# The first weight tile and x block loaded by halves from two queues, one token square on VectorE, and the up weights of two pairs kept and loaded ahead of four stores

## The chip, the core and the metric

The kernel runs on one core of a Trainium2 chip. The core has TensorE (PE in the profile; its weight loads are PEld), VectorE (DVE), ScalarE (ACT), GpSimd (POOL) and SyncE (SP), which run their own instruction streams and wait for each other by semaphores. 16 DMA engines move data for the core; SyncE and ScalarE hand them transfers through hardware queues, GpSimd through a software queue, which here carries all accumulating transfers. The metric is the device time in microseconds; lower is better. Times are medians of several runs; the profile is of one execution.

## The reference, cut to what matters

One layer of a decoder trunk over 1024 tokens of 1024 channels, in float32:

```python
h = rms_norm(x, g_mix)
z = h @ w_in + b_in                        # 1024 x 7168
va, ga, xb, gb, sa, sb = split(z)
u = silu(layer_norm(causal_conv31(va * sigmoid(ga))))
y_a = u @ w_a_out
v = rg_lru(causal_conv4(xb))
y_b = (v * gelu(gb)) @ w_b_out
x = x + (sigmoid(sa) * y_a + sigmoid(sb) * y_b) @ w_o
h = rms_norm(x, g_mlp)
f = square(relu(h @ w_1))                  # w_1: 1024 x 4096
x = x + f @ w_2
out = rms_norm(x, g_final)
```

The change touches two places: the first matmuls of `h @ w_in` with the norm ahead of them, and the passage from `@ w_o` to `h @ w_1`.

## The kernel before

**Split products.** A float32 operand is split in a high part h (rounded to the fast matmul type by a copy on ScalarE) and a low part l (the rest, by a subtraction on VectorE or by an accumulating transfer from GpSimd). A product takes three matmuls: hh, lh and hl. `split_dma` (L63) makes the low part with ScalarE (L65), an accumulating DMA on GpSimd's queue (L66) and a second ScalarE copy (L67).

**The start (L115 to L405).** Tokens come in two halves of 512 (hf 0 and 1), channels in eight blocks of 128 (c or k from 0 to 7). `xc` holds x transposed: one tile per half and pair of blocks, 512 KB each, so that `xc[0]` has the blocks 0 and 1 of the first half. `xt` holds x by tokens, eight tiles of 128 tokens, numbered t = 0 to 7; the tiles 4 to 7 (the second half) are loaded and squared first. `raw0` are the first three weight tiles (column blocks 16, 0 and 8 of w_in), 512 KB each. SyncE issues, in order: gmix (the norm's gains, 4 KB), `raw0[0]`, four tiles of xc, two more weight tiles, four of xt, four of xc, four of xt (L130 to L172). A DMA takes one of eight semaphore lanes, and the ninth waits until the first has landed.

The order on ScalarE, VectorE and TensorE is written out by hand inside `manual_schedule` (L336 to L403). TensorE runs spare passes (`idle_mm`), then for the first token half, block by block, the three products of weight tile 0. ScalarE makes the high part of each block with gmix as scale (`x_plain`, L227), VectorE the low part (`x_plain_low`, L231). Then TensorE runs weight tiles 1 and 2 on the same half. Meanwhile the tokens of the second half are squared and summed (`x_square`, L195), from which `x_root` (L202 to L210) makes 1/rms and writes it on diagonals `rd`, and four matmuls spread it over the partitions (`x_spread`, L217). That spread stands in TensorE's order behind the fifth block of weight tile 2. `x_scaled` (L221, L222) then scales the second half by it. In between VectorE works off a chain of small steps on 12 columns, the decay rates of the recurrence (`decay`, a generator; `decay_on(n)` runs n steps of it). The first half is multiplied unscaled and gets its 1/rms afterwards.

**From w_o to w_1 (GX and useq, L1773 to L1860).** Matmuls there follow Strassen-like seven-product schemes over four pairs of column blocks. `gseq` lists the steps (weight, pair i, product p): 28 for `w_a_out`, 28 for `w_o`, and, with weight "u", the products 1 and 2 of the up projection for the pairs 0 to 3 (`AHEAD` = 4); `u0` = 56 is the place of the first of those. `GX` says what else is issued at each step. After this loop `useq` runs the other up products (L1709). The weights of pair i are two raw tiles of 512 KB, `raws[i, 0]` and `raws[i, 1]`, loaded by `up_load` on SyncE (L1664). Products 1 and 2 need only `raws[i, 0]`; `g_lhs` reads it and, behind product 2, deletes the entry for the pairs 2 and 3. The loop over `useq` loads what isn't there when a pair's product 6 comes near.

In that passage GpSimd's queue carries the low parts `gu` of the up products 1 and 2 and then `o` of the others; SyncE's queue carries `x1d` (the residual, stored by rows, L1585), then the stores `fd<-f` of product 2's results (L1486), which wait for ScalarE, and the up loads.

Of the kernel before, what the change touches and what calls it, by code (L numbers as in the profile page):

```python
# [30 lines left out]
def trunk_kernel(ctx: ExitStack, tc: tile.TileContext, x, xt_in, xt_eo, vecs, w_in, w_a_out, w_b_pl, w_b_sq,  # L31
                 w_rg, w_o, w_1, w_2, g_final, out):

    nc = tc.nc
# [19 lines left out]
    HALVES = (slice(0, HS), slice(HS, S))  # L54


    def load_w(w, name):

        raw = wp.tile(list(w.shape), F32, tag="raw", name=name + "_raw")
        nc.sync.dma_start(raw, w)  # L60
        return raw
# [56 lines left out]
    wp = stage.enter_context(tc.tile_pool(name="weights", bufs=2))  # L118
# [8 lines left out]
    vec = cp.tile([P, 448], F32, name="vec")  # L127

    gmix = cp.tile([P, 16], F32, name="gmix")
    nc.sync.dma_start(gmix[:, 0:8], vecs[:, 0:8])  # L130
    nc.gpsimd.dma_start(vec, vecs)
    gmix_c = gmix[:, 0:8]
    bin_c = vec[:, 8:64]
# [11 lines left out]
    xt, xc, raw0 = [], [], []  # L145
# [6 lines left out]
    def load_xc(hf, c2):  # L152
        a = T(f"xc{hf}{c2}")
        nc.sync.dma_start(a, xt_in[hf, c2])
        xc.append(a)

    def load_w0(i):
        if i < 2:
            raw0.append(load_w(w_in[(16, 0, 8)[i]], f"w{i}"))
        else:  # L160
            raw0.append(T(f"w{i}_raw").rearrange("p (k c) -> p k c", c=P))
            nc.sync.dma_start(raw0[i], w_in[(16, 0, 8)[i]])

    load_w0(0)
    for c2 in range(4):
        load_xc(0, c2)
    load_w0(1)
    load_w0(2)
# [12 lines left out]
    def xpart(a, hf, c):  # L181
        return a[hf][c // 2][:, HALVES[c % 2]]

    rs_x = {}

    def x_square(t, eng):

        hf, i = divmod(t, 4)
        if hf not in rs_x:
            rs_x[hf] = cp.tile([P, 5, 4], F32, tag="st4", name=f"stx{hf}", bufs=2)  # L190
        a, ss = xt[(t + 4) % 8], rs_x[hf][:, 0, i:i + 1]
        if eng is nc.vector:
            nc.vector.scalar_tensor_tensor(a, a, 1.0, a, ALU.mult, ALU.mult, accum_out=ss)
        else:
            nc.scalar.activation(a, a, AF.Square, accum_out=ss)  # L195
# [16 lines left out]
    def x_spread(hf):  # L212

        rb[hf] = rb["tile"][:, HALVES[hf]]
        for i in range(4):
            d = slice(i * P, (i + 1) * P)
            nc.tensor.matmul(rb[hf][:, d], ones, rb["d"][:, d], start=True, stop=True)  # L217
# [6 lines left out]
    def x_plain(c):  # L224

        u = xc[c // 2][:, HALVES[c % 2]]
        nc.scalar.activation(xpart(xh, 0, c), u, AF.Copy, scale=gmix_c[:, c:c + 1])  # L227

    def x_plain_low(c):
        u, h = xc[c // 2][:, HALVES[c % 2]], xpart(xh, 0, c)  # L230
        nc.vector.scalar_tensor_tensor(xpart(xl, 0, c), u, gmix_c[:, c:c + 1], h.bitcast(F32),  # L231
                                       ALU.mult, ALU.subtract)
# [8 lines left out]
    w0 = []  # L241

    def first_w(i, part):
        if part == "h":
            if i < 2:
                wh = wp.tile([P, 8, P], F32R, tag="wh", name=f"w{i}_h")
                wl = wp.tile([P, 8, P], F32R, tag="wl", name=f"w{i}_l")
            else:
                wh, wl = (T(f"w{i}_{n}", F32R).rearrange("p (k c) -> p k c", c=P) for n in "hl")
            w0.append((wh, wl))  # L250
            z0.append(PS(f"z{16 + i}"))
            nc.scalar.activation(wh, raw0[i], AF.Copy)
        else:
            nc.vector.tensor_tensor(w0[i][1], raw0[i], w0[i][0].bitcast(F32), ALU.subtract)

    def first_z(i, hf, k, which):
        w, a = {"hh": (0, xh), "lh": (1, xh), "hl": (0, xl)}[which]
        nc.tensor.matmul(z0[i][:, HALVES[hf]], w0[i][w][:, k, :], xpart(a, hf, k),  # L258
                         start=k == 0 and which == "hh",
                         stop=k == 7 and which == ("hl" if i == 0 else "lh"))  # L260
# [69 lines left out]
    def decay_on(n=99):  # L330

        for _ in range(n):
            next(decaying, None)

    with tc.manual_schedule(engines={mybir.EngineType.Activation, mybir.EngineType.DVE,
                                     mybir.EngineType.PE}):  # L336
        warm = cp.tile([P, 10], F32, name="warm")
        nc.vector.memset(warm[:, 0:2], 1.0)
        nc.scalar.activation(warm[:, 0:1], warm[:, 1:2], AF.Sqrt)

        spare = PS("spare", "ps2")

        def idle_mm(n):
            for _ in range(n):
                nc.tensor.matmul(spare[:, 0:P], ones, ones, start=True, stop=True)

        idle_mm(13)
        rb["tile"] = PS("rb", "ps2")
        first_w(0, "h")
        first_w(0, "l")  # L350
        for c in range(8):
            x_plain(c)
            x_plain_low(c)
            if c == 7:
                first_w(1, "h")
                first_w(1, "l")
            for which in ("hh", "lh", "hl"):
                first_z(0, 0, c, which)
        for k in range(8):
            first_z(1, 0, k, "hh")  # L360
            first_z(1, 0, k, "hl")
        decay_on(6)
        first_w(2, "h")
        first_w(2, "l")
        decay_on(14)
        for t in range(4, 8):
            x_square(t, nc.scalar)
        for k in range(8):
            first_z(1, 0, k, "lh")
        x_root(1)  # L370
        decay_on(5)
        for k in range(8):
            first_z(2, 0, k, "hh")
            first_z(2, 0, k, "hl")
            if k == 4:
                x_spread(1)
        for k in range(8):
            first_z(2, 0, k, "lh")

        for c in range(9):  # L380
            if c < 8:
                x_scaled(1, c)
            else:
                x_root(0)
                x_spread(0)
            if 3 <= c < 7:
                x_square(c - 3, nc.scalar)
            if c:
                for which in ("hh", "lh"):
                    first_z(0, 1, c - 1, which)  # L390
                x_low(1, c - 1)
                first_z(0, 1, c - 1, "hl")
                for i in range(1, N0):
                    first_z(i, 1, c - 1, "hh")
                    first_z(i, 1, c - 1, "hl")
        for i in range(1, N0):
            for k in range(8):
                first_z(i, 1, k, "lh")
        decay()
# [295 lines left out]
    def later(ready, cost, f, *a):  # L695

        todo.append((ready, len(todo), cost, f, a))
# [89 lines left out]
    for i in range(2, NZ):  # L787
        n = zseq.index((i, 1))
# [20 lines left out]
    with tc.manual_schedule(engines=ENGINES):  # L809
        for s in range(3, NC1):  # L810
# [30 lines left out]
            c = CH[s - 1]  # L841
# [27 lines left out]
            for d in range(5):  # L869
                if s - d in EXP:  # L870
# [6 lines left out]
                    t = 3 * g + d - (2 if g < 3 else 1)  # L877
# [21 lines left out]
    wp = stage.enter_context(tc.tile_pool(name="weights2", bufs=3, reuse_waits="tile"))  # L899
# [123 lines left out]
    with tc.manual_schedule(engines=ENGINES):  # L1023
# [159 lines left out]
        for n in range(len(zseq) + 2):  # L1183
# [9 lines left out]
            if n + 3 < len(zseq):  # L1193
                i, p = zseq[n + 3]
# [15 lines left out]
    wp = early.enter_context(tc.tile_pool(name="weights3", bufs=7, reuse_waits="tile"))  # L1210
# [191 lines left out]
    def g_lhs(w, i, p):  # L1402
        if w == "u":
            src = raws[i, 0][:, 4 * (p - 1):4 * p, :]
            if p == 2 and i > 1:
                del raws[i, 0]
        elif p in (5, 6):
            src = gs[w, i][p - 5 and 1]
        else:
            src = graw[w, i, {1: 0, 2: 1, 3: 1, 7: 0, 4: 1}[p]][:, int(p == 4)]  # L1410
        go[w, i, p] = o = T(f"g{w}{i}_{p}", F32R).rearrange("p (x k c) -> p x k c", x=2, c=P)
        if w == "a" and p in (1, 2, 7):
            nc.scalar.activation(o[:, 0], src, AF.Copy)
# [242 lines left out]
    raws = {}  # L1656
# [113 lines left out]
    def g_get(n, f):  # L1770
# [32 lines left out]
        0: ((up_lhs, 0, 6), (x1_rows, 4, 5, 6, 7)),  # L1803
        1: ((x1_diag, 1),), 2: ((x1_spread, 1), (up_lhs, 1, 6)),
        3: ((x1_normed, 0, 1), (x1_normed, 1, 1), (g_t, "u", 0, 1), (g_t, "u", 1, 1)),
        4: ((g_t, "u", 0, 2), (g_t, "u", 1, 2)), 5: ((g_parts, "u", 6, 0),),
        6: ((g_parts, "u", 6, 1), (g_parts, "u", 5, 0), (up_lhs, 0, 5)),
        7: ((g_parts, "u", 5, 1), (up_lhs, 1, 5), (g_t, "u", 0, 3), (g_t, "u", 1, 3))}.items()})
    BX = {}
# [147 lines left out]
    with tc.manual_schedule(engines={mybir.EngineType.Activation, mybir.EngineType.DVE,  # L1957
                                     mybir.EngineType.PE}):
        for n in range(len(useq)):
# [4 lines left out]
            while ready < min(len(useq), n + look + 1):  # L1964
                i, p = useq[ready]
# [167 lines left out]
    with tc.manual_schedule(engines={mybir.EngineType.Activation, mybir.EngineType.DVE,  # L2133
                                     mybir.EngineType.PE}):
        for n, (g, p, kk) in enumerate(dseq[:-2]):
# [41 lines left out]
            if (g, m - 4) in XADD:  # L2177
                k = XADD[g, m - 4]
# [103 lines left out]
```

## Time and profile before

| | |
|---|---|
| median of 3 runs | 1531.3 us (1531.1 to 1531.85) |
| profiled execution, its own time | 1531.15 us |
| profiled execution, its span | 1529.4 us |
| TensorE busy, share of the span | 1519.5 us, 99% |
| granted TensorE clock, mean | 0.999 |
| DMA share of the 16 engines, 0 to 22 us | 0.92 |

The span runs from the first to the last instruction of the profiled execution; its own time has what lies around it too. A timeline row gives start and duration in us, the engine, the line, the operation, the tile written and the tiles read; in brackets stands how long the engine had been idle and what ended that. "SPq" is SyncE issuing a transfer, not the transfer. A row with x4 merges four instructions that follow each other, with the time from the first's start to the last's end. A wait for several semaphores is put down to the last.

### The profile page before, as it was taken

Reading aid. Unit: us, or ns where it says so; the run is one execution under the profiler, and the core shown is the slowest. Engines: PE = TensorE matmul, PEld = TensorE weight load, DVE = VectorE, ACT = ScalarE, POOL = GpSimd, SP = SyncE. Lnnn points to the kernel's source line nnn. Section 1 sums busy time; section 2 is a strip of 40 time slices with the busy share of each in tenths; the row PEclk is TensorE's granted clock in tenths of the full one; section 3 lists DMA queues with packets and bytes.
Section 4 is the critical chain, followed back from the end, with each engine's and each line's share of the span. In section 5 each row is a group of like instructions: output and inputs, shape, how many; then the busy total and the mean of one; then the engine's idle time right before and its main releaser. Section 6 shows DMA issues by size and latency. Waiting matters only on the chain.

```text
span 1529.4 us, 18963 instructions
## 1 busy us (share of the span) xinstructions
PE 1519.5 (99%) x6722; PEld 1251.2 (82%) x6722; DVE 1200.0 (78%) x1636; ACT 928.3 (61%) x1299; POOL 192.3 (13%) x228
## 2 busy tenths in 40 slices
PE   9999999999999999999999999999999999999998
PEld 7878887888888888888888887888888888888886
DVE  6899996998999997788869879755555387777777
ACT  6748688576566667645575777554444455545475
POOL 0111011022222222000022332000000000101010
PEclk9999999999999999999999999999999999999999
DMA  9766779797997889964879897333333974776465
GB/s 352 188 146 154 184 159 204 196 258 209 265 261 173 186 207 271 297 226 119 269 201 302 188 205 195 138 122 111 111 111 111 302 265 131 177 211 169 107 123 153
DMA packets 130799, 296.53 MB, mean 194 GB/s; under 512 B 12896, under 2 KB 34912, under 8 KB 130704
## 3 DMA queue, kind: packets, MB, share of 16 engines
q1 hardware_dynamic: 98960, 215.92, 42.0%
q0 software_dynamic: 31600, 79.15, 28.1%
q8 instruction: 52, 0.85, 0.2%
q14 instruction: 43, 0.35, 0.1%
q10 hardware_dynamic: 144, 0.26, 0.0%
HBM read 149.79 MB, written 60.82 MB: 138 GB/s over the span
## 4 chain that ended last, share of the span: by engine, by line
PE 96%; issue 2%; DVE 1%; POOL 1%; DMA 0%; ACT 0%; POOLq 0%; ACTq 0%
PE z L725 16%; PE z L258 2%; PE d1b L2002 2%; PE d2b L2002 2%; PE d0b L2002 2%; PE d3b L2002 2%; PE d0e L2002 1%; PE d3e L2002 1%; PE d3a L2002 1%; PE d2e L2002 1%; PE d2a L2002 1%; PE d1e L2002 1%; PE d1a L2002 1%; PE d0a L2002 1%; PE rg L532 1%
## 5 line engine op out<-in xcount | busy, mean ns | idle before, releaser
L725 PE MATMUL z<-xh,win_h 128*128 128x512 f32 x368 | 115.4, 391 | 0.0
L725 PE MATMUL z<-xl,win_h 128*128 128x512 f32 x368 | 114.9, 390 | 0.0
L637 DVE SCALAR_TENSOR_TENSOR y<-u,vec,y 128x511 f32<-128x511 f32 (+14 forms) x120 | 88.2, 735 | 0.0
L725 PE MATMUL z<-xh,win_l 128*128 128x512 f32 x368 | 87.4, 389 | 0.0
L637 DVE SCALAR_TENSOR_TENSOR yt<-u,vec,yt 128x511 f32<-128x511 f32 (+6 forms) x112 | 82.5, 736 | 0.0
L637 DVE SCALAR_TENSOR_TENSOR y<-yt,csum,y 128x511 f32<-128x511 f32 (+6 forms) x112 | 82.4, 736 | 0.0
L725 PEld LDWEIGHTS z<-xh,win_h 128*128 128x128 f32 x368 | 69.1, 188 | 16.0 <-ACT win_h L67 0.5
L725 PEld LDWEIGHTS z<-xl,win_h 128*128 128x128 f32 x368 | 69.1, 188 | 14.9
L725 PEld LDWEIGHTS z<-xh,win_l 128*128 128x128 f32 x368 | 69.1, 188 | 14.6
L542 ACT ACTIVATE g<-rg,vec 96x1024 f32<-96x1024 f32 x32 | 35.5, 1110 | 72.9 <-PE rg L534 72.8
L1697 ACT ACTIVATE o<-s 128x512 fp32r<-128x512 f32 x56 | 33.7, 623 | 45.7 <-DVE s L1681 26.4
L66 POOL DMA_DIRECT2D zo<-zw x45 | 39.2, 871 | 133.8 <-ACT zo L65 110.4
L483 DVE SCALAR_TENSOR_TENSOR v<-xb,vec,v 128x1023 f32<-128x1023 f32 (+2 forms) x36 | 46.2, 1282 | 6.3 <-ACT v L474 5.3
L66 POOL DMA_DIRECT2D db_10l<-br x4 | 3.5, 877 | 339.6 <-DMA br<-in_w_dram 254.4
L66 POOL DMA_DIRECT2D win_l<-win_raw x23 | 20.0, 868 | 194.0 <-ACT win_l L65 155.9
L65 ACT ACTIVATE zo<-zw 128x512 fp32r<-128x512 f32 x45 | 28.2, 626 | 24.3 <-PE z10f L929 2.1
L1219 DVE TENSOR_TENSOR o<-s,o 128x512 fp32r<-128x512 f32 x56 | 37.2, 683 | 1.3 <-ACT o L1697 1.3
L66 POOL DMA_DIRECT2D zo<-zs x30 | 26.4, 879 | 75.9 <-ACT zo L65 63.8
L67 ACT ACTIVATE zo<-zw 128x512 fp32r<-128x512 f32 x45 | 27.9, 621 | 0.0
L578 DVE TENSOR_TENSOR_SCAN g<-a,g 128x1024 f32<-128x1024 f32 x12 | 27.5, 2291 | 0.4
L66 POOL DMA_DIRECT2D ga<-gsa x8 | 7.0, 874 | 161.0 <-DMA m<-mbd 150.8
L1219 DVE TENSOR_TENSOR o<-w_raw,o 128x512 fp32r<-128x512 f32 x38 | 25.9, 683 | 0.0
(3182 smaller groups left out, 4912.0 us busy)
## 6 DMA issues: line engine op xcount, KB each, us to landing
w_raw<-in_w_dram SPq DMA_DIRECT2D x34, 512.0 KB, 5.7
br<-in_w_dram SPq DMA_DIRECT2D x32, 512.0 KB, 6.1
ar<-fd SPq DMA_DIRECT2D x32, 512.0 KB, 7.0
zw<-in_w_in_dram SPq DMA_DIRECT2D x28, 512.0 KB, 6.9
win_raw<-in_w_in_dram SPq DMA_DIRECT2D x23, 512.0 KB, 5.0
win_l<-win_raw POOLq DMA_DIRECT2D x23, 512.0 KB, 5.2
zo<-zw POOLq DMA_DIRECT2D x45, 256.0 KB, 5.7
gates<-zg SPq DMA_DIRECT2D x32, 256.0 KB, 4.1
```

The lines of the kernel that those rows point to most:

```text
L65: nc.scalar.activation(l, src, AF.Copy, scale=-1.0)
L66: nc.gpsimd.dma_start(l, src, accum_op=ALU.add)
L67: nc.scalar.activation(h, src, AF.Copy)
L258: nc.tensor.matmul(z0[i][:, HALVES[hf]], w0[i][w][:, k, :], xpart(a, hf, k), start=k == 0 and which == "hh", stop=k == 7 and which == ("hl ...
L483: nc.vector.scalar_tensor_tensor(v[:, d:S], a[:, 0:S - d], cbw_c[:, w * 12 + t:w * 12 + t + 1], v[:, d:S], ALU.mult, ALU.add)
L542: nc.scalar.activation(a, gps.pop((n, gi))[:HD, :], AF.Sigmoid, bias=(ba_c, bx_c)[gi][:, n:n + 1])
L578: nc.vector.tensor_tensor_scan(i, a, i, 0.0, ALU.mult, ALU.add)
L637: nc.vector.scalar_tensor_tensor(o[:, k:], a[:, 0:HS - k], c, o[:, k:], ALU.mult, add)
L725: nc.tensor.matmul(zps[s][:, HALVES[hf]], w[:, k, :], xw[k][part][hf], start=n == 0, stop=n == 23)
L1219: tt(l, src, h.bitcast(F32), ALU.subtract)
L1697: nc.scalar.activation(o[:, 0], src, AF.Copy)
L2002: nc.tensor.matmul(o, a, b, start=start and n == 0, stop=stop and n == len(todo) - 1, skip_group_check=not start or not stop)
```

## The change

Five edits, in the diff below:

1. gmix is no longer SyncE's first transfer. `raw0[0]` and `xc[0]` are loaded in halves (256 KB each): SyncE issues the first half of the weight tile, gmix, and the second half of the x block; ScalarE's queue the first half of the x block and the second half of the weight tile.
2. The high and low parts of weight tile 0 are made by halves (`first_half`): the first before the blocks, the second behind the high and low part of block 2.
3. 9 calls of spare matmuls in place of 13 (each is two passes in the profile).
4. Of the four token squares ahead of `x_root(1)`, t = 6 runs on VectorE; all four stand ahead of 14 steps of the decay chain, not behind them.
5. `raws[2, 0]` and `raws[3, 0]` are kept, and `raws[2, 1]` and `raws[3, 1]` are loaded at step u0 + 4, so that the loop over `useq` loads neither pair.

```diff
@@ consts, first loads
-    nc.sync.dma_start(gmix[:, 0:8], vecs[:, 0:8])
     nc.gpsimd.dma_start(vec, vecs)
...
-    load_w0(0)
-    for c2 in range(4):
+    raw0.append(wp.tile([P, 8, P], F32, tag="raw", name="w0_raw"))
+    xc.append(T("xc00"))
+    nc.sync.dma_start(raw0[0][:, 0:4], w_in[16, :, 0:4])
+    nc.scalar.dma_start(xc[0][:, HALVES[0]], xt_in[0, 0, :, HALVES[0]])
+    nc.sync.dma_start(gmix[:, 0:8], vecs[:, 0:8])
+    nc.scalar.dma_start(raw0[0][:, 4:8], w_in[16, :, 4:8])
+    nc.sync.dma_start(xc[0][:, HALVES[1]], xt_in[0, 0, :, HALVES[1]])
+    for c2 in range(1, 4):
         load_xc(0, c2)
@@ first_w, first_half
-            nc.scalar.activation(wh, raw0[i], AF.Copy)
+            if i:
+                nc.scalar.activation(wh, raw0[i], AF.Copy)
...
+    def first_half(n):
+        k = slice(4 * n, 4 * n + 4)
+        h, l = (a[:, k] for a in w0[0])
+        nc.scalar.activation(h, raw0[0][:, k], AF.Copy)
+        nc.vector.tensor_tensor(l, raw0[0][:, k], h.bitcast(F32), ALU.subtract)
@@ the written order
-        idle_mm(13)
+        idle_mm(9)
         rb["tile"] = PS("rb", "ps2")
         first_w(0, "h")
-        first_w(0, "l")
+        first_half(0)
         for c in range(8):
             x_plain(c)
             x_plain_low(c)
+            if c == 2:
+                first_half(1)
...
         first_w(2, "l")
+        for t in range(4, 8):
+            x_square(t, t == 6)
         decay_on(14)
-        for t in range(4, 8):
-            x_square(t, nc.scalar)
@@ g_lhs
             src = raws[i, 0][:, 4 * (p - 1):4 * p, :]
-            if p == 2 and i > 1:
-                del raws[i, 0]
@@ GX, step u0 + 4
-        4: ((g_t, "u", 0, 2), (g_t, "u", 1, 2)), 5: ((g_parts, "u", 6, 0),),
+        4: ((up_load, 2, (1,)), (up_load, 3, (1,)), (g_t, "u", 0, 2), (g_t, "u", 1, 2)), 5: ((g_parts, "u", 6, 0),),
```

How the instructions stand, at three places. First ScalarE at the start: `w_raw` is the raw weight tile, `w_h` its high part, `xc` the x block and `xh` its high part. Before:

```order
L339 ACT_TABLE_LOAD
L339 ACTIVATE warm<-warm 128x1
L252 ACTIVATE w_h<-w_raw 128x1024
L227 ACTIVATE xh_129<-xc_93,gmix 128x512 x2
L227 ACTIVATE xh_130<-xc_95,gmix 128x512 x2
L227 ACTIVATE xh_131<-xc_97,gmix 128x512 x2
L227 ACTIVATE xh_132<-xc_99,gmix 128x512 x2
L252 ACTIVATE w_h<-w_raw 128x1024 x2
```

And now:

```order
L166 DMA xc_91<-in_xt_dram 128x512
L168 DMA w_raw<-in_w_in_dram 128x512
L351 ACT_TABLE_LOAD
L351 ACTIVATE warm<-warm 128x1
L265 ACTIVATE w_h<-w_raw 128x512
L232 ACTIVATE xh_131<-xc_91,gmix 128x512 x2
L232 ACTIVATE xh_132<-xc_97,gmix 128x512
L265 ACTIVATE w_h<-w_raw 128x512
L232 ACTIVATE xh_132<-xc_97,gmix 128x512
L232 ACTIVATE xh_133<-xc_99,gmix 128x512 x2
L232 ACTIVATE xh_134<-xc_101,gmix 128x512 x2
L258 ACTIVATE w_h<-w_raw 128x1024 x2
```

Two DMA issues stand ahead of the table load, and half of the weight copy has moved behind the first high part of the second x tile.

Second VectorE where the token square comes in: `sm` is the decay chain, `w_l` the low part of weight tile 2, `x` a token tile and `stx` its sum of squares. Before:

```order
L284 TENSOR_SCALAR sm<-sm 128x12
L254 TENSOR_TENSOR w_l<-w_raw,w_h 128x1024
L286 SCALAR_TENSOR_TENSOR sm<-sm 128x12
L288 SCALAR_TENSOR_TENSOR sm<-sm 128x12
L290 MEMSET sm 128x12
```

And now:

```order
L296 TENSOR_SCALAR sm<-sm 128x12
L260 TENSOR_TENSOR w_l<-w_raw,w_h 128x1024
L198 SCALAR_TENSOR_TENSOR x_111,stx_247<-x_111 128x1024
L298 SCALAR_TENSOR_TENSOR sm<-sm 128x12
L300 SCALAR_TENSOR_TENSOR sm<-sm 128x12
L302 MEMSET sm 128x12
```

The square stands ahead of fourteen `sm` steps, and behind those, in both, the first step of the root (L202, now L207). On ScalarE one of four squares is gone.

Third SyncE's queue at the passage to the MLP: `x1d` is the residual by rows, `fd` the up projection's results, `w_4_raw` and `w_5_raw` the raw tiles of pair 2, `w_6_raw` and `w_7_raw` those of pair 3. Before:

```order
L1585 DMA x1d<-x1r_7845 128x1024
L1585 DMA x1d<-x1r_7863 128x1024
L1486 DMA fd<-f_0_7992 128x512
L1486 DMA fd<-f_1_8012 128x512
L1486 DMA fd<-f_2_8040 128x512
L1486 DMA fd<-f_3_8066 128x512
L1664 DMA w_4_raw<-in_w_dram 128x1024
L1664 DMA w_5_raw<-in_w_dram 128x1024
L1664 DMA w_6_raw<-in_w_dram 128x1024
L1766 DMA fd<-fa_8152 128x512
L1664 DMA w_7_raw<-in_w_dram 128x1024
L1664 DMA w_8_raw<-in_w_dram 128x1024
```

And now:

```order
L1597 DMA x1d<-x1r_7845 128x1024
L1597 DMA x1d<-x1r_7863 128x1024
L1676 DMA w_5_raw<-in_w_dram 128x1024
L1676 DMA w_7_raw<-in_w_dram 128x1024
L1498 DMA fd<-f_0_7996 128x512
L1498 DMA fd<-f_1_8016 128x512
L1498 DMA fd<-f_2_8044 128x512
L1498 DMA fd<-f_3_8070 128x512
L1676 DMA w_8_raw<-in_w_dram 128x1024
L1778 DMA fd<-fa_8156 128x512
```

Two loads stand ahead of the stores in place of four behind them; the second loads of `w_4_raw` and `w_6_raw` are gone. On TensorE and GpSimd nothing has moved but the spare matmuls that were dropped.

More of the change, by code (lines that the diff above doesn't have):

```diff
@@ L184, in trunk_kernel, with x_square @@
     rs_x = {}
-    def x_square(t, eng):
+    def x_square(t, dve=False):
         hf, i = divmod(t, 4)
@@ L191, in x_square @@
         a, ss = xt[(t + 4) % 8], rs_x[hf][:, 0, i:i + 1]
-        if eng is nc.vector:
+        if dve:
             nc.vector.scalar_tensor_tensor(a, a, 1.0, a, ALU.mult, ALU.mult, accum_out=ss)
@@ L386, in trunk_kernel @@
             if 3 <= c < 7:
-                x_square(c - 3, nc.scalar)
+                x_square(c - 3)
             if c:
```

## The prediction

> **What bounds the kernel now.** I read the page first, then the waits of TensorE's weight loads, then the timeline of the two stretches that the change touches.
>
> ```profile
> span 1529.4 us, 18963 instructions
> PE 1519.5 (99%) x6722; PEld 1251.2 (82%) x6722; DVE 1200.0 (78%) x1636; ACT 928.3 (61%) x1299; POOL 192.3 (13%) x228
> ...
> PE 96%; issue 2%; DVE 1%; POOL 1%; DMA 0%; ACT 0%; POOLq 0%; ACTq 0%
> ```
>
> TensorE is busy for 1519.5 of 1529.4 us and makes up 96% of the chain that ended last. A microsecond counts where TensorE waits, or where the change makes it wait, and almost nowhere else. These are its waits in the two places (line, what ended the wait, us in total, times, longest):
>
> ```profile
> PEld f0d L1709 <- DMA o<-s: 1.2, 1, 1.2
> PEld z L258 <- DVE xl L231: 0.8, 2, 0.5
> PEld rb L217 <- PE z L258: 0.5, 1, 0.5
> ...
> PEld gu1a L1427 <- DMA gu<-w_raw: 0.3, 1, 0.3
> ```
>
> Three are in the first 23 us, two in the step from the output projection to the MLP's up projection (near 925 and 945 us). Besides them only the wait for the first real matmul, filled with spare passes, can be won. This is the start, as the timeline has it (start, us, engine, line; in brackets the idle time before and what ended it):
>
> ```profile
> 0.74 0.39 SPq L130 DMA_DIRECT2D gmix<-in_vecs_dram  x1
> 1.18 0.42 SPq L60 DMA_DIRECT2D w_raw<-in_w_in_dram  x1
> 1.60 5.92 PE L345 MATMUL spare<-ones 128*128 128x128 f32 x26 [1.60 <-POOL ones L113]
> 4.95 1.06 ACT L252 ACTIVATE w_h<-w_raw 128x1024 fp32r<-128x1024 f32 x1 [2.72 <-DMA w_raw<-in_w_in_dram]
> 6.34 1.33 ACT L227 ACTIVATE xh<-xc,gmix 128x512 fp32r<-128x512 f32 x2 [0.34 <-DMA xc<-in_xt_dram]
> 7.17 0.70 PE L258 MATMUL z<-xh,w_h 128*128 128x512 f32 x1
> 8.12 3.88 ACT L227 ACTIVATE xh<-xc,gmix 128x512 fp32r<-128x512 f32 x6 [0.44 <-DMA xc<-in_xt_dram]
> 8.88 4.07 DVE L231 SCALAR_TENSOR_TENSOR xl<-xc,gmix,xh 128x512 fp32r<-128x512 f32 x6 [0.29 <-ACT xh L227]
> ...
> 15.17 1.22 DVE L254 TENSOR_TENSOR w_l<-w_raw,w_h 128x1024 fp32r<-128x1024 f32 x1
> 16.31 0.17 DVE L286 SCALAR_TENSOR_TENSOR sm<-sm 128x12 f32<-128x12 f32 x1
> 17.09 1.06 ACT L195 ACTIVATE x<-x 128x1024 f32<-128x1024 f32 x1 [0.15 <-DMA x<-in_x_dram]
> 18.36 1.06 ACT L195 ACTIVATE x<-x 128x1024 f32<-128x1024 f32 x1
> 18.80 0.17 DVE L293 TENSOR_TENSOR sm<-sm 128x12 f32<-128x12 f32 x1
> 19.33 0.18 ACT L195 ACTIVATION_READ_ACCUMULATOR x<-x 128x1 f32 x1
> 19.54 0.17 DVE L202 TENSOR_SCALAR stx<-stx 128x4 f32<-128x4 f32 x1 [0.58 <-ACT x L195]
> 20.98 0.39 PE L258 MATMUL z<-xl,w_h 128*128 128x512 f32 x1
> 21.47 0.97 PEld L217 LDWEIGHTS rb<-rd,ones 128*128 128x128 f32 x8 [0.52 <-PE z L258]
> ```
>
> Two things are to be seen. Transfers pace the start: ScalarE waits for x blocks at 6.34 and 8.12 and for a token square at 17.09. And at 21.47 TensorE, done with its matmuls, waits for the root of the token squares (L202 to L210), whose spread (L217) stands in its order. So what counts in the first 23 us is when that root starts, 19.54 now; 21.47 − 19.54 = 1.93 us later the spread runs. Matmuls that start earlier only wait longer there.
>
> **The start, part by part.** Gone are 0.44 us (1.18 − 0.74) in which SyncE issued the small gmix ahead of the first big transfer, and eight of the 26 spare passes (5.92/26 = 0.23 us each; 18 end near 5.7). ScalarE's queue issues two halves before its table load, where it has nothing else to do. I shift all later landings by 0.44: bytes and order stay the same. The first real matmul then comes near 5.7, not 7.17. It does not last: the second x block lands at 8.12 − 0.44 = 7.68. There the second half of the weight copy stands behind the third high part on ScalarE, and its low part on VectorE.
>
> ```profile
> L65 ACT ACTIVATE zo<-zw 128x512 fp32r<-128x512 f32 x45 | 28.2, 626 | 24.3 <-PE z10f L929 2.1
> L1219 DVE TENSOR_TENSOR o<-s,o 128x512 fp32r<-128x512 f32 x56 | 37.2, 683 | 1.3 <-ACT o L1697 1.3
> L483 DVE SCALAR_TENSOR_TENSOR v<-xb,vec,v 128x1023 f32<-128x1023 f32 (+2 forms) x36 | 46.2, 1282 | 6.3 <-ACT v L474 5.3
> ```
>
> ScalarE: 7.68 + 3.88 (six high parts) + 0.63 (the half copy, first row) = 12.2, before 8.12 + 3.88 = 12.0. VectorE ends its six low parts 0.95 behind ScalarE now (8.88 + 4.07 = 12.95), so near 13.1. The copy that was hidden in the wait for the x block is no longer hidden, and eats what the earlier transfers gave.
>
> Now the token square. VectorE goes from its last low part (12.95) to the end of w_l at 15.17 + 1.22 = 16.39 in 3.44 us; from 13.1 that is 16.6. The third token tile landed just before 17.09, with the shift 16.63. The square on VectorE costs about 1.28 (third row, the same operation on 1023 columns): 17.9. Then come the fourteen small steps of the decay chain, 18.80 + 0.17 − 16.31 = 2.66 us, which in the old order ran while ScalarE squared: 20.6. ScalarE has its three squares by 18.36 − 0.44 + 1.06 + 0.18 = 19.2, 0.3 earlier than now (19.33 + 0.18), and waits. The root starts at 20.6 instead of 19.54: **+1.1 us**. Bounds: without any shift of the transfers 21.0 (+1.5); with a shift of 0.9, since two queues may fill the engines sooner, the sum on VectorE gives about 20.1 (+0.6).
>
> Behind the spread nothing gives it back:
>
> ```profile
> 23.45 1.29 ACT L222 ACTIVATE xh<-xc 128x512 fp32r<-128x512 f32 x2 [1.70 <-DVE xc L221]
> 25.66 0.39 PE L258 MATMUL z<-xh,w_h 128*128 128x512 f32 x1
> ```
>
> TensorE needs this first high part (ready near 24.1) at 25.66, and both start from the spread; they move together.
>
> **The step to the MLP.** Two loads (the second halves of pairs 2 and 3) are issued before the four stores of fd, two reloads are dropped, and three loads leave the stretch behind 938.
>
> ```profile
> 915.02 2.29 SPq L1585 DMA_DIRECT2D x1d<-x1r  x2
> 917.24 0.95 POOL L66 DMA_DIRECT2D gu<-w_raw  x1 [5.90 <-ACT gu L65]
> ...
> q1 hardware_dynamic: 428, 1.57, 100.3%
> ...
> q0 software_dynamic: 6, 0.01, 0.9%
> ...
> 937.92 7.48 DMA o<-s
> ...
> 938.81 6.63 SPq L1664 DMA_DIRECT2D w_raw<-in_w_dram  x3
> ...
> 945.45 0.73 PE L1709 MATMUL f0d<-gu7h,o 128*128 128x512 f32 x2 [0.77 <-DMA o<-s]
> ...
> 948.01 2.77 PE f1d L1709 x12
> ...
> DMA to landing us min/median/max: 3.6/7.5/8.4
> ```
>
> The gain: the transfer of o that f0d waits for took 7.48 us beside the three loads; the quickest of its kind took 3.6 (last row, the tile o from 925 to 965 us). Without the loads it lands near 941.5, and the wait of 0.77 (matmul) to 1.2 (weight load) goes: **−1.0**.
>
> The price: SyncE is free of the x1d stores at 915.02 + 2.29 = 917.31 and issues both loads at once, beside the transfer of gu issued at 917.24, which lands just when gu1a needs it (the wait of 0.3 above). The two queue rows are from 917 to 921 us (packets, MB, share of the 16 DMA engines): in these four us the hardware queue had everything and gu's queue nothing, though gu was issued. What was queued first went first. At 1.57/4 = 0.39 MB a us, a load of 0.52 MB costs 1.33 us and both cost 2.67. Gu's issue ends at 918.19, when one load is out and the other just leaving, so I take the first wholly and half of the second ahead of it: **+2.0**. Bounds: 0, if gu goes through, and 3.9 (7.48 − 3.6), what an accumulating transfer lost behind such loads at 938. The next gu transfers each have a pass of twelve matmuls as cover (2.77 us, as in the row of f1d), and TensorE is late by then; they add nothing. The fd stores move behind the loads and have no reader until the down projection.
>
> Sum: 1.1 − 1.0 + 2.0 = +2.1 us on the profiled execution's 1531.15 (span 1529.4, the rest lies around it): 1533.25; that execution is 0.15 under the median of 1531.3. I say **1533.3**.
>
> **The rivals.** First, gu and the loads share the engines instead of queueing. Then gu, even at half speed, lands before 925 and its wait of 0.3 goes too: 1531.15 + 1.1 − 1.0 − 0.3 = 1531.0. Against it stand the two queue rows; for it, that from 938 on both kinds moved at once.
> [...]
>
> Second, the start's gain lasts: with two queues the x tiles land about 1.5 us earlier, and the root starts where ScalarE ends its squares, near 19.1 (−0.4). With the first rival's step that is 1531.15 − 0.4 − 1.3 = 1529.4. For it speaks only that the first transfers have a slow beginning (4.95 − 1.18 = 3.8 us from the issue of w_raw to its use); against it, the steady pace afterwards.
>
> Third, on the other side: the loads hold gu back as long as o was held back at 938, 3.9 us. Then 1531.15 + 1.1 − 1.0 + 3.9 = 1535.2. It decides from a delay of 3.0 us at gu1a on, since 1.1 − 1.0 + 3.0 is 0.2% (3.1 us), about what a measurement of this kernel can tell from no change. For it: packets that read from memory beside accumulating ones were slow there; against it, the smooth stores at 917.
>
> **How the numbers follow.** Forecast 0.48, sharing 0.20, lasting start 0.17, long hold 0.15. The range of 1530.0 to 1535.2 leaves out part of the second rival and little of the third. Faster by over 0.2% (under 1528.2) would need more than the second rival gives: 0.05. Slower by over 0.2% (over 1534.4) is the third and a corner of the forecast: 0.16. Within: 0.79.
>
> **What would show it.** First real matmul near 5.7, but TensorE idle again before the second x block, and the spread near 22.5 instead of 21.5; VectorE's square near 16.6 with the small steps behind it. Near 925 a wait of gu1a for a DMA of about 2.3 us; no wait of f0d near 945. The forecast is wrong if the spread comes at or before 21.5, or if gu1a waits under 1 us.

## The result and the profile after

The changed kernel takes **1535.12 us** (median; 1533.73 to 1536.91), the kernel before 1531.14 us in the same comparison (1530.6 to 1531.85). The ratio is 1.0025 with a 95% interval of 1.0016 to 1.0034: slower by 4.0 us in the medians. That is a little more than the 0.2% (3.1 us) taken as the least that can be told, though the interval reaches below it. The forecast was 1533.3, with a range up to 1535.2: the direction was right, and the result lies 0.1 us inside the end of the range. The profiled execution took 1534.44 us, with a span of 1532.7 (before 1529.4).

```profile
span 1532.7 us, 18946 instructions
PE 1520.2 (99%) x6714; PEld 1250.6 (82%) x6714; DVE 1201.5 (78%) x1639; ACT 926.8 (60%) x1298; POOL 192.3 (13%) x228
...
PE 96%; DMA 2%; DVE 1%; issue 1%; POOL 0%; ACT 0%; SPq 0%; POOLq 0%; ACTq 0%; DVEq 0%
```

The page says only that TensorE still bounds the kernel: its busy time grew by 0.7 us and the span by 3.3, so 2.6 us are added idle time. The eight spare passes that were dropped (0.23 us each, 1.8 us in all) count as busy in the kernel before, so the other matmuls were busy for about 2.5 us longer (an estimate from these figures). The waits of the changed kernel (engine, line, what ended the wait, us in total, times, longest) say where:

```profile
PEld z L270 <- ACT xh L232: 2.1, 2, 1.6
PEld gu3a L1439 <- DMA gu<-w_raw: 1.7, 1, 1.7
...
PEld gu1a L1439 <- DMA gu<-w_raw: 1.0, 1, 1.0
```

The wait of f0d for o (1.2 us before) is gone, as forecast. In its place stand two waits for gu, and a wait in the first nine microseconds.

The sign that the prediction gave for its own failing, a wait of gu1a under 1 us, is met on the matmul and just missed on the weight load (1.00 us). The delay that it put wholly at gu1a came for the most part later, at gu3a:

```profile
928.11 0.73 PE L1439 MATMUL gu1a<-gu2h,gu 128*128 128x512 f32 x2 [0.58 <-DMA gu<-w_raw]
935.26 0.72 PE L1439 MATMUL gu3a<-gu2h,gu 128*128 128x512 f32 x2 [1.27 <-DMA gu<-w_raw]
```

The start of the changed kernel, in rows picked from its timeline:

```profile
4.28 0.63 ACT L265 ACTIVATE w_h<-w_raw 128x512 fp32r<-128x512 f32 x1 [1.12 <-DMA w_raw<-in_w_in_dram]
5.62 0.73 PE L270 MATMUL z<-xh,w_h 128*128 128x512 f32 x1
7.41 0.72 ACT L232 ACTIVATE xh<-xc,gmix 128x512 fp32r<-128x512 f32 x1 [1.84 <-DMA xc<-in_xt_dram]
8.18 0.50 PE L270 MATMUL z<-xh,w_h 128*128 128x512 f32 x1 [1.27 <-ACT xh L232]
8.91 0.72 ACT L232 ACTIVATE xh<-xc,gmix 128x512 fp32r<-128x512 f32 x1 [0.78 <-DMA xc<-in_xt_dram]
17.89 1.23 DVE L198 SCALAR_TENSOR_TENSOR x<-x 128x1024 f32<-128x1024 f32 x1 [0.29 <-DMA x<-in_x_dram]
19.16 1.06 ACT L200 ACTIVATE x<-x 128x1024 f32<-128x1024 f32 x1 [1.40 <-DMA x<-in_x_dram]
21.61 0.16 DVE L207 TENSOR_SCALAR stx<-stx 128x4 f32<-128x4 f32 x1
23.56 1.13 PE L222 MATMUL rb<-rd,ones 128*128 128x128 f32 x8 [0.26 <-DVE rd L213]
```

The first real matmul came at 5.62 (forecast 5.7, before 7.17). Then TensorE waited: ScalarE got the second half of the first x tile at 7.41 and the second tile at 8.91; for the second tile 7.68 was forecast, and 8.12 was the old value. The token square on VectorE began at 17.89 (forecast 16.6). The root starts at 21.61 (forecast 20.6, before 19.54) and the spread at 23.56 (22.5, before 21.50). That is 2.06 us late, and it is never won back: at the weight gu0a near 907 TensorE is 2.08 us behind the old kernel.

### The profile page after: what moved, and what is told of

The parts are those of the page before. It is cut to its first block, busy times and chain, and to the rows that moved or that the text cites. A ratio compares the mean times of both kernels' runs of the same rounds, so it can differ in the third digit from the quotient of the medians.

```text
span 1532.7 us, 18946 instructions
## 1 busy us (share of the span) xinstructions
PE 1520.2 (99%) x6714; PEld 1250.6 (82%) x6714; DVE 1201.5 (78%) x1639; ACT 926.8 (60%) x1298; POOL 192.3 (13%) x228
## 4 chain that ended last, share of the span: by engine, by line
PE 96%; DMA 2%; DVE 1%; issue 1%; POOL 0%; ACT 0%; SPq 0%; POOLq 0%; ACTq 0%; DVEq 0%
PE z L739 16%; PE d2b L2014 2%; PE d1b L2014 2%; PE d0b L2014 2%; PE d3b L2014 2%; PE d0e L2014 1%; PE d3a L2014 1%; PE d2e L2014 1%; PE d2a L2014 1%; PE d1e L2014 1%; PE d1a L2014 1%; PE d0a L2014 1%; PE d3e L2014 1%; PE z L270 1%; PE rg L546 1%; PE rg L548 1%
```

## The experiments

Each changes either the start or the step to the MLP, mostly beside the kernel before. "Ratio" is to the kernel before on the same chip, with its 95% interval; differences in us are between medians.

### The two places apart

The step alone (edit 5 in the kernel before):

```diff
-            if p == 2 and i > 1:
-                del raws[i, 0]
...
-        4: ((g_t, "u", 0, 2), (g_t, "u", 1, 2)), 5: ((g_parts, "u", 6, 0),),
+        4: ((up_load, 2, (1,)), (up_load, 3, (1,)), (g_t, "u", 0, 2), (g_t, "u", 1, 2)), 5: ((g_parts, "u", 6, 0),),
```

> Before, with the two early up loads and the kept tiles alone (edit 5); the start is that of before. In the changed kernel's trace TensorE lost about 2.6 us near 925 to 938 to transfers of gu and won the wait of f0d (1.05 us) back. Theory 'the loads hold up gu': the same here, so the span is +1.3 to +1.6 us over before, with waits of gu1a and gu3a for DMA and none of f0d. Rival 'the changed medians are 4.0 us apart, of which the start is only 2.07': the MLP step costs +1.9. Rival 'gu and loads share the engines': -1.3. The prediction's own terms: +1.0, all of it at gu1a, none at gu3a.

1533.63 against 1531.43, ratio 1.0012 (1.0003 to 1.0021): +2.2 us. The start alone (the changed kernel with these lines put back):

> The changed kernel without edit 5: only the start is changed. If the start's delay of 2.07 us at the spread (23.56 in place of 21.50) is never won back, the span and the median are +2.07 over before. Rival 'given back later': under +1.5. With the run of edit 5 alone the two should add up to the whole, +3.3 in spans, +4.0 in medians.

1532.99, ratio 1.0009 (1.0000 to 1.0018): +1.6 us. The two add up to 3.8 of the 4.0 us. So both parts seem to cost time by themselves, though the start's interval just reaches 1; which of them costs more, these intervals do not tell.

### The step: which loads, and when

The kept tiles (the lines with `del` taken out) are in every run of this section. The trace of the step alone shows two prices. Its execution took 1534.67 us, 1.0 above the median of that kernel, so it shows more than the usual price. The first is the wait. The rows are the DMA queues of the kernel before, from 922 to 927 us (packets, MB, share of the 16 engines):

```profile
q0 software_dynamic: 490, 0.90, 106.9%
q1 hardware_dynamic: 17, 0.05, 2.8%
```

and of the kernel with the step alone:

```profile
q1 hardware_dynamic: 299, 1.08, 59.1%
q0 software_dynamic: 143, 0.27, 44.4%
```

Before, the accumulating transfers of gu and o have the engines to themselves in these five microseconds and move 0.90 MB. With the two loads, SyncE's queue has more than half and they move 0.27 MB. That is a mean of different things. The changed kernel's trace, where these five microseconds look alike (57.4% and 45.0%), parts them: from 921 to 923 SyncE's queue had everything (101.0% and 100.5% in the two microseconds) and gu's almost nothing (1.2%, then none), as in the prediction's rows, though a transfer of gu had been issued at 919.33; from 923 to 927 now one and now the other had more; from 927 to 929 each had about half (51% and 53% for SyncE's, 58% and 56% for GpSimd's). Sharing did not make the loads free, though: the engines were full already (a DMA share of 1.03 from 917 to 922 in the kernel before, 1.10 from 922 to 927), and every transfer of gu that was still in the queue came later. The time from issue to landing of the three transfers of gu from 913 to 926 (shortest, median, longest), before and with the step alone:

```profile
DMA to landing us min/median/max: 6.7/6.7/8.0
```
```profile
DMA to landing us min/median/max: 10.3/10.4/11.9
```

The same transfers in the order of their issue, read one by one; the first is the one that gu1a waits for, the third the one for gu3a:

```
kernel before       8.0   6.7   6.7
step alone         10.4  10.3  11.9
changed kernel      8.7   9.0  10.7
```

The hold grows along the queue: 2.4, 3.6 and 5.2 us with the step alone, and only 0.7, then 2.3 and 4.0 in the changed kernel's profile. So gu1a had little to wait for there and gu3a much.

The second price is the clock. TensorE's rows (start, us) in the kernel with the step alone, and the window from 927 to 932 (busy us of the five engines, then granted clock, DMA share, GB/s):

```profile
925.98 0.39 PE L1425 MATMUL gu1a<-gu2l,gu 128*128 128x512 f32 x1
928.60 1.22 PE L1425 MATMUL gu1a<-gu2h,gu 128*128 128x512 f32 x2 [2.23 <-DMA gu<-w_raw]
929.62 0.63 PE L1425 MATMUL gu1a<-gu2l,gu 128*128 128x512 f32 x1
930.04 1.05 PE L1425 MATMUL gu1a<-gu2h,gu 128*128 128x512 f32 x2
```
```profile
927.00:932.00 5.00, 3.40 (x8) 2.71 (x9) 5.00 (x5) 1.27 (x2) 0.00 (x0) 0.66 1.09 272
```

After a wait of 2.23 us a matmul follows another at 0.43 us (930.04 − 929.62 = 0.42) and not at 0.23, until 932. Ahead of this wait TensorE was 0.95 us behind the kernel before in this trace, at gu2a 4.75: 3.8 us are lost, though the wait was 2.2. The changed kernel's profile paid the first price only; its clock in the same stretch is 1.00:

```profile
927.00:932.00 5.00, 4.42 (x20) 3.14 (x19) 5.00 (x6) 2.77 (x4) 0.00 (x0) 1.00 1.09 270
932.00:937.00 5.00, 3.73 (x17) 2.75 (x16) 5.00 (x6) 4.94 (x8) 0.87 (x1) 1.00 0.48 142
```

How often the second price is paid is known only indirectly. Of the eleven executions of the step alone, the seven that took 1533.52 us or more have a granted clock of 0.998 over the whole span, the four that took 1533.07 or less 0.999; in the kernel before both values occur with no difference in time (medians 1531.34 at 0.998, 1531.49 at 0.999).

One load in place of two:

```diff
-        4: ((g_t, "u", 0, 2), (g_t, "u", 1, 2)), 5: ((g_parts, "u", 6, 0),),
+        4: ((up_load, 2, (1,)), (g_t, "u", 0, 2), (g_t, "u", 1, 2)), 5: ((g_parts, "u", 6, 0),),
```

> Before, with the kept tiles and one early load only, that of pair 2, at the changed kernel's place ahead of the stores; pair 3's half is loaded where the loop over the other products asks for it. Theory 'gu is held back by the bytes ahead of it': half the delay, gu1a waits about 1.4 us in place of 2.7 and TensorE's clock stays up behind so short a wait; with the wait of f0d gone in part (two loads fewer near 938) the sum is +0.2 to +0.6. Rival 'the first load alone holds gu': +1.5 to +2.2 as with both.

1531.68 against 1531.44, ratio 1.0001 (0.9992 to 1.0010): +0.2 us, the median that "held back by the bytes ahead" gave. Its trace does not show that theory's wait of 1.4 us with the clock up: the executions go from 1530.25 to 1533.5, the profiled one took the longest, and there one load was enough for a wait of gu1a of 1.97 us and a clock of 0.66 behind it. That the loads are cheap in executions whose clock stays up fits both runs, but no trace of a shorter execution of either shows it.

Both loads behind the first of the four stores, and behind the second:

```diff
-        ... 5: ((g_parts, "u", 6, 0),),
+        ... 5: ((g_parts, "u", 6, 0), (up_load, 2, (1,)), (up_load, 3, (1,))),
```
```diff
-        6: ((g_parts, "u", 6, 1), (g_parts, "u", 5, 0), (up_lhs, 0, 5)),
+        6: ((g_parts, "u", 6, 1), (g_parts, "u", 5, 0), (up_lhs, 0, 5), (up_load, 2, (1,)), (up_load, 3, (1,))),
```

> Before, with the kept tiles and both early loads, but issued behind the first of the four stores fd (near 926.5, when the third transfer of gu has been queued) in place of ahead of it. Theory 'the loads cost only by what they are ahead of': gu1a waits no longer than before, at most gu3a by about 1 us; the wait of f0d (1.05) goes; 0 to -1.0. Rival 'any early load costs as much, since it comes among accumulating transfers anyway': +1.5 to +2.2 as in the run of edit 5 alone.

> The same behind the second store (near 931), between the last transfer of gu and the first of o. Theory 'only by what they are ahead of': no wait of any gu, the transfers of o find the queues free from 934.5 on, the wait of f0d goes: -1.0. Rival 'any early load costs as much': +1.5 or more. Rival 'the waits move on': f0b or f1b waits for o about 1 us, no difference in the end.

Behind the first: 1530.25, ratio 0.9991 (0.9982 to 1.0000), −1.2 us. Behind the second: 1531.57, ratio 1.0001 (0.9992 to 1.0009), no difference. The DMA share (the last number but one) shows why the first place is good. The kernel before, from 922 to 937, and then the kernel with the loads behind the first store:

```profile
922.00:927.00 5.00, 5.00 (x23) 3.90 (x22) 5.00 (x7) 2.38 (x5) 1.09 (x2) 1.00 1.10 191
927.00:932.00 5.00, 5.00 (x23) 4.12 (x22) 5.00 (x7) 3.63 (x5) 0.00 (x0) 1.00 0.35 114
932.00:937.00 5.00, 5.00 (x23) 4.14 (x23) 5.00 (x5) 4.97 (x9) 1.47 (x2) 1.00 0.46 110
```
```profile
927.00:932.00 5.00, 5.00 (x24) 4.14 (x23) 5.00 (x7) 3.70 (x5) 0.00 (x0) 1.00 1.02 268
```

Between 927 and 932 the engines of the kernel before are two thirds empty (0.35). A load issued at 926.6 (in the kernel before the first store is issued at 926.28, in 0.3 us) falls into that hole, one issued near 918 falls into the full stretch ahead of it (1.03 and 1.10). Behind the second store the loads meet the first transfers of o, and the waits move on to VectorE, which makes f0d's operand:

```profile
DVE s L1683 <- DMA o<-s: 1.7, 1, 1.7
PEld f0d L1707 <- DVE gu7l L1219: 1.4, 1, 1.4
...
PE f0d L1707 <- DVE gu7l L1219: 1.0, 1, 1.0
```

So "the waits move on" is what happened there, on another operand than named. Last, no early load at all, only the `if` and its `del` taken out:

> Before, with the kept tiles alone: two reloads fewer, no early load; the second halves of the pairs 2 and 3 are loaded where the loop over the other products asks for them (near 939 and later). Tells what of the -1.2 of the loads behind the first store comes from the dropped reloads. Theory 'bytes beside o': two loads of the three stay near 938.8 and 945, so that half of the gain, -0.3 to -0.6, is there. Rival 'the place is what counts': within 0.2 of before. Rival 'the reloads were all of it': -1.2.

1529.96 against 1531.15, ratio 0.9991 (0.9983 to 1.0000): **−1.2 us**, as much as with the loads at their best place. "The reloads were all of it" fits the median, and the wait is gone without any early load; the interval alone would not shut out the half gain. Its span, and the rows of f0d on TensorE and of SyncE's loads (the last row merges two loads and the wait between them):

```profile
span 1527.9 us, 18963 instructions
```
```profile
943.81 0.39 PE L1707 MATMUL f1c<-gu5h,o 128*128 128x512 f32 x1
944.04 0.39 PE L1707 MATMUL f0d<-gu7h,o 128*128 128x512 f32 x1
944.26 0.39 PE L1707 MATMUL f0d<-gu7l,o 128*128 128x512 f32 x1
944.49 0.61 PE L1707 MATMUL f0d<-gu7h,o 128*128 128x512 f32 x2
...
938.38 0.32 SPq L1484 DMA_DIRECT2D fd<-f  x1
942.41 4.98 SPq L1662 DMA_DIRECT2D w_raw<-in_w_dram  x2
```

f0d runs without a bracket: it waits for nothing. With the reload gone, SyncE's first load is issued at 942.41 and not at 938.81. The transfers of o issued from 933 to 950 took 5.5 us from issue to landing there (median; 3.6 to 6.8), where the one that f0d needs took 7.5 before. Issued at 937.92 as before, it would land near 943.4 with the 5.5, nearly through when the load comes (an estimate from these figures).

### The start: square, loads, clock

The token square on VectorE and the order of the decay steps alone (edit 4 in the kernel before):

```diff
-        decay_on(14)
-        for t in range(4, 8):
-            x_square(t, nc.scalar)
+        for t in range(4, 8):
+            x_square(t, nc.vector if t == 6 else nc.scalar)
+        decay_on(14)
```

> Before, with edit 4 alone: the square of token tile 6 on VectorE, all squares ahead of the fourteen decay steps; loads, spare passes and weight copies as before. Theory 'VectorE's order sets the root': the square starts at the landing of the tile (17.1), ends near 18.4, the fourteen steps of 2.65 us end near 21.0, the root starts there and not at 19.54: +1.45 us in the root, the spread and the median. Rival 'the square takes load off ScalarE': root at 19.5, no difference.

1532.33 against 1531.44, ratio 1.0007 (0.9998 to 1.0016): +0.9 us. In its trace the square ran where forecast and the root starts at 20.85, 1.31 us later than before; the spread waits for it:

```profile
17.12 1.23 DVE L193 SCALAR_TENSOR_TENSOR x<-x 128x1024 f32<-128x1024 f32 x1 [0.70 <-DMA x<-in_x_dram]
20.85 0.17 DVE L202 TENSOR_SCALAR stx<-stx 128x4 f32<-128x4 f32 x1
...
22.80 1.13 PE L217 MATMUL rb<-rd,ones 128*128 128x128 f32 x8 [1.41 <-DVE rd L208]
```

That the median moved by less than the spread fits a second observation: the shifted work meets the loads near 940 at another moment. In this trace TensorE waited 0.2 us for o at f0d, before 0.8, and the span grew by 0.9 us where the spread came 1.3 later. The edit changes two things, the engine of the square and the place of the fourteen steps, and no run parts them; from the rows of the kernel before, a square behind the steps would end near 20.2 (18.80 + 0.17 + 1.23), an estimate that is still behind 19.54. Now the start with this edit undone, then also with 13 calls of spare matmuls:

```diff
-        for t in range(4, 8):
-            x_square(t, t == 6)
         decay_on(14)
+        for t in range(4, 8):
+            x_square(t)
```
```diff
-        idle_mm(9)
+        idle_mm(13)
```

> The start of the changed kernel, but with all four token squares on ScalarE and behind the fourteen decay steps, as before; up loads as before. VectorE is then free near 20.3 and ScalarE ends its squares near 20.4, so the root starts near 20.5 and not 21.61. Theory 'two limits tied' (TensorE came to the spread only at 23.3 by itself, kept by the gap before the second x block and by a granted clock of 0.57 from 9 to 13 us): only 0.26 us is won, +1.8 over before, and the spread waits for TensorE, not for the root. Rival 'VectorE alone sets it': 1.1 us is won, +0.95 over before, spread near 22.45.

> As the run before it, with 13 calls of spare matmuls (26 passes, up to 7.6 us) and not 9: TensorE is kept busy through part of the gap. Theory 'two limits tied, and the idle gap brings the clock down': the granted clock from 9 to 13 us is near 1 again, TensorE reaches the spread near 22.5, the root (20.5) allows it near 22.45: +1.05 over before. Rival 'the clock has nothing to do with the gap': clock near 0.57 again, no gain, +1.8. Rival 'VectorE alone': no gain over the run before it.

1532.06, ratio 1.0004 (0.9996 to 1.0013), and 1531.47, ratio 1.0000 (0.9991 to 1.0009): +0.6 and 0.0. The first lies 0.9 us under the start alone (1532.99), as much as this edit costs by itself. Root and spread of the first of them, and of the start alone:

```profile
20.11 0.17 DVE L207 TENSOR_SCALAR stx<-stx 128x4 f32<-128x4 f32 x1 [0.16 <-ACT x L200]
...
22.36 1.05 PE L222 MATMUL rb<-rd,ones 128*128 128x128 f32 x8
```
```profile
20.66 0.16 DVE L207 TENSOR_SCALAR stx<-stx 128x4 f32<-128x4 f32 x1
...
22.61 1.13 PE L222 MATMUL rb<-rd,ones 128*128 128x128 f32 x8 [0.80 <-DVE rd L213]
```

"Two limits tied" does not hold in general. In the start alone the spread waited 0.80 us for the root, so VectorE set it; in the changed kernel's profile it waited 0.26, since TensorE itself was late; with the squares on ScalarE it waited for nothing. What made TensorE late in the changed kernel's profile is seen in its windows (PEclk is the last number but two):

```profile
5.00:9.00 4.00, 2.68 (x10) 1.53 (x9) 2.11 (x3) 1.38 (x3) 0.00 (x0) 1.00 0.98 335
9.00:13.00 4.00, 3.78 (x9) 2.63 (x10) 3.33 (x6) 4.00 (x7) 0.00 (x0) 0.57 1.02 419
```

After a stretch that was a third idle the mean clock was 0.57 for four microseconds. In the other two traces of this start with 9 calls it was 1.00 there, so the longer warm-up's gain (0.6 us in the medians, inside the intervals) is not shown to be the clock.

Why did the first transfers not land earlier? First the halves through SyncE's queue alone, then whole tiles from two queues, each with 13 calls and the squares on ScalarE:

```diff
-    nc.scalar.dma_start(xc[0][:, HALVES[0]], xt_in[0, 0, :, HALVES[0]])
+    nc.sync.dma_start(xc[0][:, HALVES[0]], xt_in[0, 0, :, HALVES[0]])
...
-    nc.scalar.dma_start(raw0[0][:, 4:8], w_in[16, :, 4:8])
+    nc.sync.dma_start(raw0[0][:, 4:8], w_in[16, :, 4:8])
```
```diff
-    nc.sync.dma_start(raw0[0][:, 0:4], w_in[16, :, 0:4])
-    nc.scalar.dma_start(xc[0][:, HALVES[0]], xt_in[0, 0, :, HALVES[0]])
+    nc.sync.dma_start(raw0[0], w_in[16])
+    nc.scalar.dma_start(xc[0], xt_in[0, 0])
     nc.sync.dma_start(gmix[:, 0:8], vecs[:, 0:8])
-    nc.scalar.dma_start(raw0[0][:, 4:8], w_in[16, :, 4:8])
-    nc.sync.dma_start(xc[0][:, HALVES[1]], xt_in[0, 0, :, HALVES[1]])
```

> As the run with 13 calls of spare matmuls and all squares on ScalarE, but ScalarE's queue issues nothing: all five first transfers (halves, gmix) go through SyncE's queue, in the same order. In four profiles with halves from two queues the second x tile landed at 7.95, 8.68, 8.80 and 8.89, in six with whole tiles from one queue between 7.99 and 8.22; the last token tile 18.18 to 19.13 against 18.23 to 18.46. Theory 'two queues cost': 8.1 here, the token tile 18.3, median -0.3 to -0.6 against the run with two queues. Theory 'halves cost' (twice the packets of 2 KB): 8.7 and 18.9, no difference in the median. As it is one profile, only a clear value counts.

> The same with whole tiles (512 KB), from two queues: SyncE the weight tile and gmix, ScalarE the x tile. Theory 'two queues cost': the second x tile lands near 8.7 and the last token tile near 18.9. Theory 'halves cost': 8.1 and 18.3. In either case the first real matmul comes near 7.5, since the weight tile's copy waits for the whole tile.

1532.65, ratio 1.0010 (1.0001 to 1.0019), and 1531.5, ratio 1.0002 (0.9993 to 1.0012). ScalarE's waits with one queue:

```profile
5.92 0.72 ACT L232 ACTIVATE xh<-xc,gmix 128x512 fp32r<-128x512 f32 x1 [2.01 <-DMA gmix<-in_vecs_dram]
7.88 0.72 ACT L232 ACTIVATE xh<-xc,gmix 128x512 fp32r<-128x512 f32 x1 [1.24 <-DMA xc<-in_xt_dram]
9.15 0.72 ACT L232 ACTIVATE xh<-xc,gmix 128x512 fp32r<-128x512 f32 x1 [0.55 <-DMA xc<-in_xt_dram]
```

The start of the high part for which the second x tile was waited for, in every trace of these starts:

```
whole tiles, one queue (kernel before)                       8.12
whole tiles, two queues                                      8.46
halves, two queues, five traces      7.93  7.98  8.70  8.82  8.91
halves, one queue                                            9.15
```

"Two queues cost" falls, by one trace: with one queue the halves came latest, 1.0 us behind the whole tiles, and the first high part waited 2.01 us for gmix, which now stands among large transfers. With two queues they came now as early as before, now 0.6 to 0.8 us later. Which of the halves, gmix's place and the transfer of vec from GpSimd decides that is open.

### All mended

The changed kernel with the loads behind the first store, the squares as before and 13 calls:

> The changed kernel with its three costly steps mended: both early loads behind the first store fd, all token squares on ScalarE behind the decay steps, 13 calls of spare matmuls; halves from two queues stay. If start and up projection add: -1.2 from the loads' place and 0 to +0.5 from the start, so 1530.2 to 1530.8, faster than the changed kernel by over 4 us but not than the before kernel with the loads' place alone.

1530.67, ratio 0.9997 (0.9987 to 1.0006): 4.4 us under the changed kernel, and not to be told from the kernel before. The best found is the kernel before with the `if` and its `del` taken out, at 1529.96; its interval just reaches 1.

## Why the prediction came out as it did

Both mechanisms were forecast with their signs, and the forecast was still 1.8 us short. By the medians 1.4 us of this are the loads' price (3.4 in place of 2.0) and 0.5 the start (1.6 in place of 1.1); the gain (1.2 in place of 1.0) takes 0.2 back. These are differences near what can be told at all. The three steps that failed, as the prediction put them:

**"So I take the first wholly and half of the second ahead of it: +2.0."** The loads' price is the difference between the step alone (+2.2) and the kept tiles alone (−1.2): 3.4 us. That is close to the upper bound of 3.9, so by the medians the third rival (long hold, 1535.2) described the step better than the forecast. The changed kernel's own profile, of an execution 0.7 us under its median, shows 2.4 us: TensorE is 2.11 us behind the kernel before at gu0a (924.19 − 922.08) and 4.50 at f0d (948.56 − 944.06). There the size was nearly right and the place was not: 0.7 us was lost at gu1a, which with the step alone waited 2.2 us as forecast (2.3), and 1.6 at gu3a. Two things were missing. The delay was priced as the bytes queued ahead of one transfer; the queueing came, but behind it both queues shared full engines (about half each from 927 to 929 in the changed kernel), and the later transfers came later still. And behind the wait of 2.2 us TensorE's clock was down (0.66 from 927 to 932): +1.6 us in the step-alone trace (3.8 − 2.2), nothing in the changed kernel's profile.

**"The next gu transfers … add nothing."** gu3a waited 1.3 to 1.7 us in the changed kernel. A pass is as long as said, but it was not all cover: in the kernel before the second and third transfer landed about 1.4 and 1.5 us ahead of the weight loads that need them (919.87 + 6.7 against 927.97, 922.45 + 6.7 against 930.69). And the hold grows along the queue as long as the loads last: the last transfer of gu took 11.9 us with the step alone and 10.7 in the changed kernel, where it took 6.7 before.

**"I shift all later landings by 0.44: bytes and order stay the same."** The second x tile came at 7.93 to 8.91 in the five traces of this start, never at 7.68; in the changed kernel's profile it was 0.8 us late (8.91 − 8.12). The chain on VectorE behind it was right: the square and the fourteen steps put the root 1.31 us later by themselves (working without a shift: +1.5). With the start alone the spread came 1.11 us late, the very term of the sum (+1.1), but that is luck in part, since the landings happened to be early there, and 2.06 us late in the changed kernel's profile, where they were late and TensorE slow. In the medians the start costs 1.6 instead of 1.1.

Right was that f0d's wait goes: TensorE won 1.06 us there in every trace with the kept tiles, except with the loads behind the second store. But the prediction gave this to three loads leaving the stretch. It is the dropped reloads; loading the rest early added a price and no gain that these runs can tell.

The first rival had the sharing right from 927 on, and its result wrong; the second (the start's gain lasts) fell, since no x tile came 1.5 us earlier. The size of the error lay in one habit: each delay was priced at the first instruction that meets it, though the queue behind it, and in the step-alone trace the clock, go on paying.

## What to carry to other kernels

Before an early load is called free, read the DMA share of the stretch into which it falls, not of the one out of which it is taken: by the medians the same two loads cost 3.4 us near 918, where the engines were full (1.03 from 917 to 922), and nothing at 926.6, ahead of a stretch at 0.35. Count the transfers dropped apart from the transfers moved, and try the dropping alone. And where an engine that sets the end waits for a long dependent chain (here a root behind small steps), an operation that is moved to another engine must not stand ahead of small steps that used to be hidden there: the square and the order together put the root 1.31 us later here.

## What the hardware showed that was not expected

TensorE fell to half rate after short waits, which the prediction did not reckon with, and not always: after waits of 2.23 and 1.97 us matmuls of 512 columns followed each other at 0.43 instead of 0.23 us for up to 3.4 us (928.6 to 932.0); after waits of 0.58 and 1.27 us in the changed kernel's MLP step they did not. At its start, though, behind a wait of also 1.27 us (8.18) and with TensorE busy for 67% of the time from 5 to 9, they did (0.43 us from 10.28 on, 10.71 − 10.28). The length of the wait alone does not tell these cases apart: 1.27 us stands on both sides. What does, no run shows.

The same first loads, executed again, had ScalarE begin on the second x tile anywhere from 7.93 to 8.91, while with whole tiles from one queue the tile had landed between 7.99 and 8.22 in six traces (the author's reading ahead of the run with one queue). And SyncE needed 2.1 and 1.1 us to issue the two early loads in the changed kernel (at 919.51 and 921.8), where the issue of such a load at 938.81 in the kernel before took 0.33, though the engines were full there too (54.0% and 51.6% for the two queues from 938 to 944). What made the issue long no run shows. The same two loads in the kernel with the step alone, in one row:

```profile
918.43 3.34 SPq L1662 DMA_DIRECT2D w_raw<-in_w_dram  x2
```
